# Values by 512-column products, and the scan branch's gates computed with features on partitions and turned back

## The chip, the cores and the metric

The kernel runs on one core of a Trainium2 chip. The time is the device time of one execution in microseconds (us). The profile has five engines: the tensor engine (PE, with its weight loads shown apart as PEld), the vector engine (DVE), the scalar engine (ACT), GpSimd (POOL) and the queue that issues transfers (SP). PSUM is the memory that the tensor engine writes its products to, in banks of 128 x 512 floats.

## The reference, cut to what matters

Three residual blocks run one after the other on one sequence of 1024 steps with 1024 features. The change touches one product in the first and one in the third:

```python
# block 1
u = jnp.einsum('bsd,de->bse', x, w_in) + b_in
q, k, v, z_att, glu_a, glu_b, z_conv, g_att, g_conv = jnp.split(u, _split_points(), axis=-1)
att = stick_breaking_attention(heads(q), heads(k), heads(v)).reshape(B, S, D_ATT)
c = glu_a * jax.nn.sigmoid(glu_b)
c = causal_depthwise_conv(c, conv_w, conv_b)          # 31 taps
...
# block 3
proj = hn @ w_in[i]
u_s5, z_s5, z_ssd, xBC, dt_raw = jnp.split(proj, SPLITS, axis=-1)
y_s5 = s5_branch(...) * jax.nn.silu(z_s5)
y_ssd = ssd_branch(xBC, dt_raw, z_ssd, ...)           # conv, chunked scan, y * silu(z_ssd), norm over groups of 256
h = h + jnp.concatenate([y_s5, y_ssd], axis=-1) @ w_out[i]
```

`v` has 512 features, `z_ssd` has 1024 in four groups of 256.

## The kernel before

All products are made in float32 accuracy from two parts of each operand, `hi` and `lo`, with three matmuls for each block of 128 features: hi x hi, hi x lo, lo x hi. A product over the 1024 features is therefore a chain of 24 matmuls into one PSUM bank. A weight comes by a transfer into `wraw` (2 buffers), ACT rounds it to `whi` (L146) and POOL subtracts to get `wlo` (L147); both have 3 buffers.

The usual product is `Core.dense`: a tile of 128 weight features is the stationary operand, half of time (512 steps) the moving one, so the result has features on partitions and time in the columns. All these matmuls stand under L156. `evac` takes the result out of PSUM, and `K.tick()` then writes the next steps of the background work into the program. Two products are made the other way round, with the activation as the stationary operand and time on partitions: the values `v` of block 1 (`projections`, L597, evacuated by DVE at L599) and the gates of block 3's scan branch (`SSD.rest`, L1670, evacuated by ACT at L1673 as `szt`, with a tanh into `zth` and the DVE operation L1676). Both run over 256 columns of weights at a time.

In `projections` the background work is the convolution over 31 taps: each tap is one DVE operation over 128 x 1024 (L568 on `co`). The stage runs over the convolution's inputs (evacuated at L557), q and k, then V, then two sets of gates (L608).

In block 3, the function `block3` goes through four groups g. The scan of a group (`SSD.scan`, 8 chunks of 128 steps) is written with high priority ahead of `SSD.project(g + 1)`, which makes the next group's inputs: `conv_in` (products, then a convolution of 4 taps on DVE, L1631 to L1639), then `rest`: the gates and the turning of the inputs (`xt`, `bt`) to time on partitions (transposes L1649). A chunk of the scan goes from POOL (`sg`, L1705) to PE (L1707), ACT (`M`), DVE (L1714), PE (L1720), DVE (L1723, L1727, L1728), POOL (L1742); the state passes through L1725. At a group's end DVE forms a norm (L1745, L1748), and for the first three groups `leaves` turns the result (four `turned` calls of 4 transposes, L1762), scales it by ACT into the one buffer `mo` (L1771) and sends it to memory (L1772). After the third group `glu` starts: it loads `gy` tiles (L1902; 2 buffers, tag "cp", which `conv_in` uses too), ACT and DVE split them (L70, L71), and products follow at L156.

All PE transposes write to the tag "tp", which has two PSUM banks. A bank is taken in the order in which the program is written, so a transpose written later can't take a bank ahead of one written earlier.

Of the kernel before, what the change touches and what calls it, by code (L numbers as in the profile page):

```python
# [26 lines left out]
def parts(x, bits):  # L27
    """x as three floats, the first two short enough that small multiples of them are exact."""
    a = float(np.float32(math.floor(x * 2.0 ** bits) / 2.0 ** bits))
    b = float(np.float32(math.floor((x - a) * 2.0 ** (bits + 10)) / 2.0 ** (bits + 10)))  # L30
    return a, b, float(np.float32(x - a - b))
# [14 lines left out]
class Act:  # L46
    """An activation, features on partitions, as float32r parts: n tiles, each by halves of time."""
# [14 lines left out]
    def scaled(self, k, h, src, scale, early=None):  # L62
        """The parts of src * scale, one factor for each feature. early: (t, a, b) with a t + b = src * scale, known before src."""
# [10 lines left out]
class Core:  # L74
    """Pools, constants and the pieces that all three blocks share."""
# [31 lines left out]
    def activation(self):  # L107
        """The activation that the products read next, in the place of the one before."""
        return Act(self, 8, "y", self.ypools)
# [19 lines left out]
    def weight(self, src, a, b, eng=None):  # L129
        """A weight tile [128, a, b] as two float32r parts that add up to it."""  # L130
# [5 lines left out]
    def warm(self, n):  # L136
        """Products of ones that keep the tensor engine's clock up until the first operands are there."""
# [11 lines left out]
    def mm3(self, ps, w, x, half, first=True, last=True, cols=slice(None)):  # L149
        """ps += sum over the k-tiles of w[k].T @ x[k] over one half of time or its columns cols, in float32 from the parts."""  # L150
# [16 lines left out]
    def dense(self, srcs, x, evac, group=1):  # L167
        """evac(index, half, psum) for each 128-feature tile of the product."""
        self.dense_list([(src, lambda hf, ps, i=i: evac(i, hf, ps)) for i, src in enumerate(srcs)], x, group)

    def dense_list(self, items, x, group=1):
        """evac(half, psum) for each (weight, evac); a group of tiles takes the first half of time, then the second."""
# [13 lines left out]
    def dense_half(self, srcs, x, evac, h, cols=slice(0, HALF), eng=None):  # L186
        """One half of time, or its columns cols, for all tiles; evac(index, psum)."""
# [9 lines left out]
    def tick(self):  # L197
        """Trace the next steps of the work that runs beside the products."""
# [7 lines left out]
    def tables(self, name):  # L206
        """From here on the activations that need a table use this set; those traced earlier go first."""
# [8 lines left out]
    def act(self, out, in_, func, **kw):  # L216
        """An activation with a function that not every table set has."""
# [5 lines left out]
    def in_turn(self, ins):  # L223
        """Keeps a step of the work that hooks trace behind the products that were traced before."""
# [4 lines left out]
    def rsqrt(self, pool, v, n):  # L229
        """v ** -0.5 for a small [128, n] tile, by Newton's iteration."""  # L230
# [15 lines left out]
    def exp(self, pool, x):  # L246
        """x = exp(x) in place for a small tile: 2 ** n from the exponent's bits, the rest from tanh."""
# [18 lines left out]
    def score_bank(self):  # L266
        """Three banks for attention scores where nothing needs sums over the features."""
# [3 lines left out]
    def stat_bank(self):  # L271
        """A bank for sums over the features; beside the attention's steps they have one of their own."""
# [4 lines left out]
    def col_sums(self, ps, at, accs, n=4):  # L277
        """ps[:, at + b] = the sum over partitions and tiles of acc[:, 128 b : 128 b + 128]."""
# [5 lines left out]
    def spread(self, pool, col, tag, n=4, bufs=2):  # L284
        """[128, n] with time on partitions -> [128, 128 n], the same row on each partition."""
# [8 lines left out]
    def inverse_rms(self, pool, accs, eps, dim, n=4):  # L294
        """(mean square + eps) ** -0.5 over the features, time on partitions."""
# [7 lines left out]
class Squares:  # L303
    """Squares of tiles added up, in two chains on two engines."""
# [23 lines left out]
class Norm:  # L328
    """h * g in parts, for products that take the norm's factor for each time step afterwards."""
# [18 lines left out]
def block1(K, hold, g0, then):  # L348
    """Returns h, the norm that block 2 starts from and what then(h, norm) gave, traced beside the end. hold: an ExitStack for what stays open."""
# [48 lines left out]
    if True:  # L398
        pl = left(el, "pl")
        lng, lnb = K.const("ln_g", (128, 8), pool=pl), K.const("ln_b", (128, 8), pool=pl)  # L400
        with ExitStack() as em:
# [43 lines left out]
            def finish(hf, engines=None):  # L445
                """Steps of the layer norm in place, and the next norm's factor: the mean of (r c g + b) ** 2 from sums over c g c g and 2 c g b."""
# [49 lines left out]
class LayerNorm:  # L496
    """(t - mean) * (variance + eps) ** -0.5 over the features, step by step for one stretch of time."""
# [40 lines left out]
def projections(K, pa, bin_, x, v):  # L538
    """The inputs of the convolution, the convolution itself, values and gates."""
# [47 lines left out]
    for c in range(2):  # L587
        wa, wb = K.weight(I["w_v"][c, 0], 4, 256), K.weight(I["w_v"][c, 1], 4, 256)
        for tb in range(8):
            ps = K.mm_bank()  # L590
            n = 0
            for k in range(8):
                wh, wl = (wa, wb)[k // 4]
                xh, xl = x.at(k, tb // 4)
                ts = slice(tb % 4 * 128, (tb % 4 + 1) * 128)
                for a, b in ((xh, wh), (xl, wh), (xh, wl)):
                    nc.tensor.matmul(ps[:, :256], a[:, ts], b[:, k % 4, :], start=n == 0, stop=n == 23)  # L597
                    n += 1
            nc.vector.tensor_add(v[:, tb, c * 256:(c + 1) * 256], ps[:, :256], bv[:, c * 256:(c + 1) * 256])  # L599
# [18 lines left out]
def conv_branch(K, pb):  # L618
    """What remains of the convolution's branch before its product, as steps that run beside the attention."""
# [168 lines left out]
def merge(K, pm, pz, m, cz, az):  # L788
    """m = the two branches' products, each under its gate."""
# [27 lines left out]
def even(K, h, norm, pe):  # L817
    """Traces the first tiles of the layer, for the first half of time; returns what traces the others."""
# [1324 lines left out]
```

## Time and profile before

| | |
|---|---|
| median of 3 runs | 3303.04 us |
| lowest and highest run | 3298.67, 3305.75 us |
| span of the profiled execution | 3303.1 us |
| PE busy | 3150.4 us, 95% |
| DVE busy | 2130.6 us, 65% |
| POOL busy | 1468.9 us, 44% |
| ACT busy | 1110.7 us, 34% |

The profiled execution agrees with the median. Its times are counted from the start of the span. A row "L597 <- wlo, x70h 128x256" is an instruction written at line 597 that reads these two tiles; "x3" are three in a row; the text in square brackets is the idle time of the engine just before, and what ended it. PE's matmuls are pipelined: the duration shown is longer than the step from one start to the next.

### The profile page before, as it was taken

The numbers are of one execution on the slowest core, as the hardware profiler recorded it, in microseconds if no ns is written. First come the engines' busy times: TensorE is split into PE (matmuls) and PEld (weight loads), VectorE is DVE, ScalarE is ACT, GpSimd is POOL, SyncE is SP. The second block draws the span as 40 slices with busy tenths as digits, with TensorE's granted clock in tenths as the row PEclk, the third lists the DMA queues.
The fourth block names the chain that finished last, engine by engine and source line by source line (L and its number), as shares of the span: only waits on it lengthen the run. The fifth ranks groups of instructions, "written<-read, shape, count | busy, mean of one in ns | idle before, by whom it ended". The sixth has DMA issues, their size and how long they took to land. (4 is left out here: it accounts for less than half of the span.)

```text
span 3303.1 us, 41709 instructions
## 1 busy us (share of the span) xinstructions
PE 3150.4 (95%) x15689; PEld 2522.8 (76%) x15689; DVE 2130.6 (65%) x3382; ACT 1110.7 (34%) x1974; POOL 1468.9 (44%) x1128
## 2 busy tenths in 40 slices
PE   9999999999989999999999999999999879989997
PEld 7877677778768888777777777787777768778886
DVE  8986887663773462232287777766955988874444
ACT  3025556553341121111144334521112323423343
POOL 2322332225644446777543222541214665794455
PEclk9999999999989999999999999999989999989999
DMA  3132122134311122122121111364253232365322
GB/s 128 52 107 78 68 77 76 47 136 140 110 64 45 42 69 68 56 89 75 51 74 42 42 36 65 135 190 127 88 130 93 76 104 71 118 223 182 115 91 100
DMA packets 159738, 303.95 MB, mean 92 GB/s; under 512 B 23840, under 2 KB 66864, under 8 KB 159536
## 3 DMA queue, kind: packets, MB, share of 16 engines
q1 hardware_dynamic: 149104, 294.96, 27.4%
q10 hardware_dynamic: 10368, 6.30, 0.9%
q8 instruction: 124, 2.03, 0.3%
q14 instruction: 78, 0.64, 0.1%
q0 software_dynamic: 64, 0.03, 0.0%
HBM read 236.59 MB, written 64.62 MB: 91 GB/s over the span
## 5 line engine op out<-in xcount | busy, mean ns | idle before, releaser
L147 POOL TENSOR_TENSOR wlo<-wraw,whi 128x1024 fp32r<-128x1024 f32 (+1 forms) x305 | 751.5, 2466 | 1086.2 <-ACT whi L146 1037.2
L146 ACT CAST whi<-wraw 128x1024 fp32r<-128x1024 f32 (+1 forms) x309 | 307.9, 998 | 806.4 <-PE mm L156 593.3
L568 DVE SCALAR_TENSOR_TENSOR co<-cpad,conv_w,co 128x1024 f32<-128x1024 f32 x120 | 180.3, 1543 | 0.9
L156 PE MATMUL mm<-mixh,whi 128*128 128x512 f32 x256 | 99.3, 393 | 2.1 <-DVE h L927 2.1
L156 PE MATMUL mm<-mixh,wlo 128*128 128x512 f32 x256 | 99.7, 391 | 0.0
L156 PE MATMUL mm<-mixl,whi 128*128 128x512 f32 x256 | 99.7, 391 | 0.0
L1636 DVE SCALAR_TENSOR_TENSOR h<-cp,conv_w,h 128x512 f32<-128x512 f32 x96 | 95.3, 993 | 3.3
L218 ACT ACTIVATE e<-e 128x128 f32<-128x128 f32 (+7 forms) x128 | 84.5, 681 | 33.5 <-DVE e L758 32.6
L762 DVE TENSOR_TENSOR_SCAN e<-e 128x128 f32<-128x128 f32 (+7 forms) x64 | 93.3, 1466 | 0.7
L927 DVE TENSOR_TENSOR h<-h,mm 128x512 f32<-128x512 f32 x64 | 43.3, 680 | 59.3 <-PE mm L156 59.3
L761 DVE TENSOR_TENSOR e<-e,z 128x128 f32<-128x128 f32 (+7 forms) x64 | 53.9, 851 | 37.3 <-ACT e L218 37.2
L320 DVE TENSOR_TENSOR sq<-sq,sq 128x512 f32<-128x512 f32 (+1 forms) x46 | 54.0, 1174 | 29.8 <-ACT sq L319 28.9
L1956 DVE TENSOR_TENSOR h<-h,mm 128x512 f32<-128x512 f32 x32 | 21.9, 684 | 76.2 <-PE mm L156 76.2
L832 DVE TENSOR_TENSOR sz<-mm,row 128x512 f32<-128x512 f32 x32 | 22.0, 689 | 75.0 <-PE mm L156 75.0
L218 ACT ACTIVATE z<-z 128x128 f32<-128x128 f32 (+7 forms) x64 | 43.3, 683 | 75.7 <-DVE z L763 75.6
L1720 PE MATMUL tp<-xd,M 128*128 128x64 f32 x256 | 38.6, 298 | 30.7 <-DVE M L1714 28.6
L1720 PEld LDWEIGHTS tp<-xd,M 128*128 128x128 f32 x256 | 36.0, 212 | 39.0 <-DVE M L1714 26.5
L916 DVE TENSOR_TENSOR cv<-mm,cv 128x512 f32<-128x512 f32 x16 | 11.1, 691 | 81.4 <-PE mm L156 81.4
L319 ACT ACTIVATE sq<-h 128x512 f32<-128x512 f32 x60 | 37.7, 629 | 72.2 <-POOL h L1988 29.7
L156 PE MATMUL mm<-y00h,whi 128*128 128x512 f32 x138 | 56.5, 410 | 3.9 <-DVE zt L1795 3.3
L1041 POOL TENSOR_TENSOR sw<-sw,rope_s 128x512 f32<-128x512 f32 x18 | 28.5, 1583 | 69.9 <-DVE sw L1040 65.9
L156 PEld LDWEIGHTS mm<-mixh,whi 128*128 128x128 f32 x256 | 48.1, 188 | 14.3 <-DVE h L927 2.8
(1524 smaller groups left out, 10533.7 us busy)
## 6 DMA issues: line engine op xcount, KB each, us to landing
wraw<-w_in SPq DMA_DIRECT2D x76, 512.0 KB, 3.6
wraw<-w_in_even SPq DMA_DIRECT2D x53, 512.0 KB, 3.5
wraw<-w_in_odd SPq DMA_DIRECT2D x22, 512.0 KB, 3.5
sp_g<-gt SPq DMA_DIRECT2D x32, 256.0 KB, 2.0
g<-sp_g SPq DMA_DIRECT2D x32, 256.0 KB, 3.1
wraw<-w_out SPq DMA_DIRECT2D x16, 512.0 KB, 3.4
wraw<-w_out_even SPq DMA_DIRECT2D x32, 256.0 KB, 2.6
wraw<-w_out_odd SPq DMA_DIRECT2D x16, 512.0 KB, 3.6
```

The source lines that it names most:

```text
L146: self.nc.scalar.copy(hi, src)
L147: (eng or self.nc.gpsimd).tensor_sub(lo, src, hi.bitcast(F32))
L156: ins = self.nc.tensor.matmul(ps, a[:, k, :], b[:, cols], start=first and n == 0, stop=last and n == total - 1).ins
L218: ins = self.nc.scalar.activation(out, in_, func, **kw).ins
L319: nc.scalar.activation(sq, src, AF.Square, scale=scale)
L320: (nc.vector if self.count > 5 else self.engines[i]).tensor_add(self.accs[i], self.accs[i], sq)
L568: nc.vector.scalar_tensor_tensor(o, cpad[:, tap:tap + S], cw[:, j, tap:tap + 1], o, op0=ALU.mult, op1=ALU.add)
L761: nc.vector.tensor_tensor(e[:, :L], e[:, :L], z[:, :L], op=ALU.max)
L762: nc.vector.tensor_tensor_scan(e[:, rev], e[:, rev], e[:, rev], 0.0, op0=ALU.add, op1=ALU.bypass)
L927: nc.vector.tensor_add(h[e][:, half(hf)], h[e][:, half(hf)], ps)
L1636: nc.vector.scalar_tensor_tensor(oh, c(d), cw[:, ch, 3 - d:4 - d], oh, op0=ALU.mult, op1=ALU.add)
L1720: nc.tensor.matmul(yp[:, i * 64:(i + 1) * 64], M[:, i, :], xd[:, i * 64:(i + 1) * 64], start=True, stop=True)
```

## The change

1. **Values.** The weights of V are laid out as four pieces of 256 input features by 512 output features. All four pieces, in both parts, stay in a pool of their own (`vw`). Eight products of 24 matmuls over 512 columns take the place of sixteen over 256. A product is evacuated by one DVE operation over 512 columns, followed by two `K.tick()`.
2. **Gates.** `rest` makes the gates with `K.dense`, two tiles of 128 features by two halves of time. For each of the four results ACT copies PSUM to `zf` (tag "cp"), PE turns it with 4 transposes into a "tp" bank, ACT takes the four blocks out with the time factor `zc`, then one tanh and one DVE operation over 512 columns follow. Buffers of the tags "cp" and "th" are used; `zth` is gone.
3. Docstrings are removed, which shifts line numbers. In block 3 a line of before is 6 lines further down in the changed kernel (L1762 is L1768, L1725 is L1731); the V product is at L603, the gates' transposes at L1674.

```diff
-    for c in range(2):
-        wa, wb = K.weight(I["w_v"][c, 0], 4, 256), K.weight(I["w_v"][c, 1], 4, 256)
+    with K.pool("vw") as vw:
+        wv = []
+        for q in range(4):
+            raw = K.wp.tile([128, 2, 512], F32, tag="wraw", name=K.n("wraw"), bufs=2)
+            hi, lo = (vw.tile([128, 2, 512], F32R, name=K.n("wv")) for _ in range(2))
+            nc.sync.dma_start(raw, I["w_v"][q])
+            K.split_into(raw, hi, lo)
+            wv.append((hi, lo))
         for tb in range(8):
             ps = K.mm_bank()
...
-                    nc.tensor.matmul(ps[:, :256], a[:, ts], b[:, k % 4, :], start=n == 0, stop=n == 23)
+                    nc.tensor.matmul(ps, a, b, start=n == 0, stop=n == 23)
                     n += 1
-            nc.vector.tensor_add(v[:, tb, c * 256:(c + 1) * 256], ps[:, :256], bv[:, c * 256:(c + 1) * 256])
+            nc.vector.tensor_add(v[:, tb, :], ps, bv)
+            K.tick()
             K.tick()
...
         sz = pool.tile([128, 8, 256], F32, tag="szt", name=K.n("szt"), bufs=2)
-        wz = [K.weight(K.I["w_z_3"][g, i], 4, 256) for i in range(2)]
-        for tb in range(8):
...
-                for p, q in ((xh, wh), (xl, wh), (xh, wl)):
-                    nc.tensor.matmul(ps[:, :256], p[:, ts], q[:, k % 4, :], start=n == 0, stop=n == 23)
-                    n += 1
-            z = sz[:, tb, :]
-            nc.scalar.activation(z, ps[:, :256], AF.Copy, scale=self.zc[:, tb:tb + 1])
-            t2 = pool.tile([128, 256], F32, tag="zth", name=K.n("zth"), bufs=2)
-            K.act(t2, z, AF.Tanh)
-            nc.vector.scalar_tensor_tensor(z, t2, 1.0, z, op0=ALU.add, op1=ALU.mult)
+
+        def ev(i, hf, ps):
+            z = self.pc.tile([128, 4 + HALF], F32, tag="cp", name=K.n("zf"), bufs=2)[:, 0:HALF]
+            nc.scalar.copy(z, ps)
+            pt = K.tp_bank()
+            for k in range(4):
+                nc.tensor.transpose(pt[:, k * 128:(k + 1) * 128], z[:, k * 128:(k + 1) * 128], K.ident)
+            o = sz[:, 4 * hf:4 * hf + 4, i * 128:(i + 1) * 128]
+            for k in range(4):
+                nc.scalar.activation(o[:, k, :], pt[:, k * 128:(k + 1) * 128], AF.Copy, scale=self.zc[:, 4 * hf + k:4 * hf + k + 1])
+            t2 = self.pc.tile([128, HALF], F32, tag="th", name=K.n("th"), bufs=2).rearrange("p (a b) -> p a b", b=128)
+            K.act(t2, o, AF.Tanh)
+            nc.vector.scalar_tensor_tensor(o, t2, 1.0, o, op0=ALU.add, op1=ALU.mult)
             K.tick()
+
+        K.dense([K.I["w_z_3"][2 * g + i] for i in range(2)], y, ev)
```

The change moves instructions at three places. POOL, first block, the weight splits around V: `wlo` are the splits of q's, k's and the gates' weights, and the two pairs wlo_774, wlo_780 and wlo_1027, wlo_1033 of before are V's. First before, then after, where V's are called `wv`.

```order
22 L147 TENSOR_TENSOR wlo_708<-wraw_706,whi_707 128x1024
23 L147 TENSOR_TENSOR wlo_774<-wraw_772,whi_773 128x1024
24 L147 TENSOR_TENSOR wlo_780<-wraw_778,whi_779 128x1024
25 L147 TENSOR_TENSOR wlo_1027<-wraw_1025,whi_1026 128x1024
26 L147 TENSOR_TENSOR wlo_1033<-wraw_1031,whi_1032 128x1024
```

```order
21 L147 TENSOR_TENSOR wlo_642<-wraw_640,whi_641 128x1024
22 L147 TENSOR_TENSOR wv_777<-wraw_775,wv_776 128x1024
23 L147 TENSOR_TENSOR wlo_708<-wraw_706,whi_707 128x1024
24 L147 TENSOR_TENSOR wv_783<-wraw_781,wv_782 128x1024
25 L147 TENSOR_TENSOR wv_789<-wraw_787,wv_788 128x1024
26 L147 TENSOR_TENSOR wv_795<-wraw_793,wv_794 128x1024
```

All four splits are still there, but the first now stands ahead of the last split before V, and all four stand ahead of V's first product.

PE, third block, the end of the second group's scan. Before, the first eight of the sixteen transposes of `leaves` (from `szt`) stand behind the start of a product; 21 matmuls of this product follow, then four transposes, eight matmuls of the next product and the last four transposes. These rows are the last two sets of transposes and what stands between them:

```order
11611 L1762 MATMUL tp_21649<-ident,szt_21033 128x128 x4
11612 L156 MATMUL mm_22792<-y01h_17411,whi_22730 128x512
11613 L156 MATMUL mm_22792<-y01l_17412,whi_22730 128x512
11614 L156 MATMUL mm_22792<-y01h_17411,wlo_22731 128x512
11615 L156 MATMUL mm_22792<-y11h_17415,whi_22730 128x512
11616 L156 MATMUL mm_22792<-y11l_17416,whi_22730 128x512
11617 L156 MATMUL mm_22792<-y11h_17415,wlo_22731 128x512
11618 L156 MATMUL mm_22792<-y21h_17419,whi_22730 128x512
11619 L156 MATMUL mm_22792<-y21l_17420,whi_22730 128x512
11620 L1762 MATMUL tp_21657<-ident,szt_21033 128x128 x4
```

After, behind the scan's last state product (L1731, row 11089) and four more rows like the first:

```order
11094 L1768 MATMUL tp_21276<-ident,szt_20753 128x128
11095 L1768 MATMUL tp_21285<-ident,szt_20753 128x128
11096 L1768 MATMUL tp_21276<-ident,szt_20753 128x128
11097 L1768 MATMUL tp_21285<-ident,szt_20753 128x128
11098 L1768 MATMUL tp_21293<-ident,szt_20753 128x128 x4
11099 L1768 MATMUL tp_21301<-ident,szt_20753 128x128 x4
11100 L1674 MATMUL tp_21690<-ident,zf_21688 128x128 x4
11101 L1674 MATMUL tp_21751<-ident,zf_21749 128x128 x4
11102 L156 MATMUL mm_22262<-y01h_17207,whi_22222 128x512
11103 L156 MATMUL mm_22262<-y01l_17208,whi_22222 128x512
```

The products between the transposes are gone: all sixteen transposes of `leaves` now follow each other, then eight of the next group's gates (`zf`), and only then a product. At the first group's end the order is the same but for seven matmuls ahead of L1768.

PE, third block, the end of the third group's scan in the changed kernel (L1726 and L1731 are scan steps; the product at 11425 is the first of `glu`; L1656 turns the fourth group's inputs):

```order
11416 L1731 MATMUL tp_22141<-st_22120,h_6307 128x256
11417 L1713 MATMUL aux_22855<-sg_22859,after_17710 128x512
11418 L1726 MATMUL tp_22178<-xd_22176,M_22169 128x64 x4
11419 L1674 MATMUL tp_22603<-ident,zf_22601 128x128 x4
11420 L1674 MATMUL tp_22664<-ident,zf_22662 128x128 x4
11421 L1674 MATMUL tp_22731<-ident,zf_22729 128x128 x4
11422 L1731 MATMUL tp_22178<-st_22157,h_6307 128x256
11423 L1674 MATMUL tp_22770<-ident,zf_22768 128x128 x4
11424 L1656 MATMUL tp_22784<-ident,h_6310 128x128 x4
11425 L156 MATMUL mm_23276<-y00h_23173,whi_23271 128x512
```

The last gate product of the fourth group ends at row 11409; from there to row 11425 PE has scan steps and transposes only. In the kernel before, `glu`'s products stand between the steps of the third scan.

## Rows read from the trace of the kernel before

**Rows 1.** Busy time by stretches of the span: length, then for each engine busy us (instructions), PE's granted clock, share and rate of the DMA engines.

```profile
94.90:153.70 58.80, 51.99 (x384) 51.05 (x384) 57.33 (x55) 4.20 (x4) 15.01 (x5) 0.88 0.16 54
153.70:233.00 79.30, 77.76 (x339) 62.57 (x337) 78.94 (x59) 15.91 (x21) 22.93 (x8) 1.00 0.26 90
2504.70:2873.10 368.40, 323.58 (x1840) 278.81 (x1840) 316.34 (x435) 124.59 (x250) 236.91 (x215) 0.95 0.26 88
```

**Rows 2.** Timeline of PE, instructions in order of start: start, duration, line, tiles. First and last of 8 matmuls of V that follow each other, first and last of 22 over 512 columns, and four transposes as one row.

```profile
109.76 0.28 PE L597 MATMUL mm<-wlo,x70h 128*128 128x256 f32 x1
110.60 0.28 PE L597 MATMUL mm<-whi,x20h 128*128 128x256 f32 x1
...
227.78 0.39 PE L156 MATMUL mm<-x01h,wlo 128*128 128x512 f32 x1
232.55 0.39 PE L156 MATMUL mm<-x71h,wlo 128*128 128x512 f32 x1
...
2660.47 0.60 PE L1649 MATMUL tp<-ident,h 128*128 128x128 f32 x4
```

**Rows 3.** The V stage and what follows: waits of PE from 94.9 to 153.8 us (total, times, longest); then timelines of DVE, of POOL, and of DVE and PE at the stage's end.

```profile
PE mm L597 <- POOL wlo L147: 3.6, 1, 3.6
PE mm L597 <- DVE v L599: 3.1, 2, 2.3
...
108.90 3.67 DVE L568 SCALAR_TENSOR_TENSOR co<-cpad,conv_w,co 128x1024 f32<-128x1024 f32 x3
128.57 3.07 DVE L568 SCALAR_TENSOR_TENSOR co<-cpad,conv_w,co 128x1024 f32<-128x1024 f32 x1
...
124.38 6.18 POOL L147 TENSOR_TENSOR wlo<-wraw,whi 128x1024 fp32r<-128x1024 f32 x2 [20.71 <-ACT whi L146]
...
232.22 1.40 DVE L608 SCALAR_TENSOR_TENSOR gt<-mm,b_in,gs 128x512 f32<-128x512 f32 x2
233.02 0.50 PE L156 MATMUL mm<-x00h,whi 128*128 128x512 f32 x1
```

**Rows 4.** DVE's groups of instructions by line and shape, in the projections (94.9 to 233 us) and in block 3's scans (2500 to 2985 us): count, total us, mean ns, idle time before them.

```profile
L568 DVE SCALAR_TENSOR_TENSOR co<-cpad,conv_w,co 128x1024 f32<-128x1024 f32 x80 | 122.6, 1571 | 0.4
L599 DVE TENSOR_TENSOR v<-mm,b_v 128x256 f32<-128x256 f32 x16 | 6.7, 417 | 1.4 <-PE mm L597 1.3
...
L1676 DVE SCALAR_TENSOR_TENSOR szt<-zth,szt 128x256 f32<-128x256 f32 x32 | 26.0, 816 | 10.5 <-ACT zth L218 10.3
L1639 DVE SCALAR_TENSOR_TENSOR h<-th,h 128x512 f32<-128x512 f32 x24 | 22.5, 936 | 3.7 <-ACT th L218 3.6
```

**Rows 5.** The end of the first two groups. For group 0 the scan's last state products, the transposes of `leaves` and DVE's L1748; then ACT's `mo` operations of group 0 and of group 1 (min/median/max ns, first and last start); one product of PE behind the idle time; and busy time by stretches as in rows 1, for groups 0 and 1.

```profile
L1725 PE MATMUL tp<-st,h x14: 377/379/634, 2565.9 to 2630.5; 128*128 128x256 f32 x14
L1762 PE MATMUL tp<-ident,szt x16: 270/273/476, 2643.8 to 2658.0; 128*128 128x128 f32 x16
2641.21 6.42 DVE L1748 TENSOR_SCALAR szt<-szt,rsq 128x256 f32<-128x256 f32 x8
L1771 ACT ACTIVATE mo<-tp,ssd_norm_w x4: 673/690/691, 2649.2 to 2661.4; 128x512 f32<-128x512 f32 x4
L1771 ACT ACTIVATE mo<-tp,ssd_norm_w x4: 669/690/692, 2772.5 to 2781.8; 128x512 f32<-128x512 f32 x4
2647.72 0.78 PE L156 MATMUL mm<-y00l,whi 128*128 128x512 f32 x1
...
2643.00:2661.00 18.00, 15.31 (x71) 12.60 (x72) 12.83 (x19) 5.07 (x8) 5.11 (x6) 0.91 0.47 160
2769.80:2782.00 12.20, 12.20 (x65) 10.21 (x64) 11.11 (x15) 3.77 (x7) 2.70 (x3) 1.00 0.30 108
```

**Rows 6.** First scan step on PE of groups 1 and 2 (first and last start of 16).

```profile
L1711 PE MATMUL tp<-h,h x16: 272/275/527, 2677.8 to 2748.3; 128*128 128x128 f32 x16
L1711 PE MATMUL tp<-h,h x16: 270/275/377, 2797.1 to 2852.1; 128*128 128x128 f32 x16
```

**Rows 7.** The third group's end: busy time of L71 alone (DVE, the splits of `gy`) from 2504.7 to 2873.1 us; the `gy` transfers; the scan's last state products and its norm L1745; the first `glu` products; and busy time by stretches as in rows 1.

```profile
2504.70:2873.10 368.40, 17.98 (x16) 0.95 0.26 88
L1902 SPq DMA_DIRECT2D gy<-sp_yg x16: 319/319/320, 2812.4 to 2867.3; - x16
DMA to landing us min/median/max: 2.4/2.5/2.6
L70 ACT ACTIVATE y00h<-gy x1: 619/619/619, 2829.0 to 2829.0; 128x512 fp32r<-128x512 f32 x1
L70 ACT ACTIVATE y70h<-gy x1: 632/632/632, 2847.1 to 2847.1; 128x512 fp32r<-128x512 f32 x1
L1725 PE MATMUL tp<-st,h x14: 377/379/483, 2820.2 to 2865.4; 128*128 128x256 f32 x14
L1745 DVE TENSOR_SCALAR ssv<-ss x1: 173/173/173, 2873.1 to 2873.1; 128x8 f32<-128x8 f32 x1
2854.43 0.40 PE L156 MATMUL mm<-y00h,whi 128*128 128x512 f32 x1
...
2865.40:2880.00 14.60, 12.56 (x62) 9.60 (x61) 11.15 (x25) 7.45 (x12) 6.65 (x4) 1.00 0.56 189
2880.00:2955.00 75.00, 65.89 (x298) 52.81 (x296) 51.35 (x63) 24.73 (x43) 67.33 (x55) 0.89 0.66 220
2955.00:2990.00 35.00, 35.00 (x164) 29.15 (x164) 22.87 (x37) 10.66 (x18) 25.64 (x16) 1.00 0.61 196
```

More of the change, by code (lines that the diff above doesn't have):

```diff
@@ L585, in projections @@
     K.dense_list(items[2:], x)
-    for c in range(2):
-        wa, wb = K.weight(I["w_v"][c, 0], 4, 256), K.weight(I["w_v"][c, 1], 4, 256)
+    with K.pool("vw") as vw:
[6 more added lines that the diff above has]
+            wv.append((hi, lo))
         for tb in range(8):
             ps = K.mm_bank()
+            ts = slice(tb % 4 * 128, (tb % 4 + 1) * 128)
             n = 0
             for k in range(8):
-                wh, wl = (wa, wb)[k // 4]
-                xh, xl = x.at(k, tb // 4)
-                ts = slice(tb % 4 * 128, (tb % 4 + 1) * 128)
+                wh, wl = (w[:, k % 2, :] for w in wv[k // 2])
+                xh, xl = (t[:, ts] for t in x.at(k, tb // 4))
                 for a, b in ((xh, wh), (xl, wh), (xh, wl)):
-                    nc.tensor.matmul(ps[:, :256], a[:, ts], b[:, k % 4, :], start=n == 0, stop=n == 23)
+                    nc.tensor.matmul(ps, a, b, start=n == 0, stop=n == 23)
                     n += 1
-            nc.vector.tensor_add(v[:, tb, c * 256:(c + 1) * 256], ps[:, :256], bv[:, c * 256:(c + 1) * 256])
+            nc.vector.tensor_add(v[:, tb, :], ps, bv)
+            K.tick()
             K.tick()
@@ L1660, in rest @@
         sz = pool.tile([128, 8, 256], F32, tag="szt", name=K.n("szt"), bufs=2)
-        wz = [K.weight(K.I["w_z_3"][g, i], 4, 256) for i in range(2)]
-        for tb in range(8):
-            ps = K.mm_bank()
-            n = 0
-            for k in range(8):
-                wh, wl = wz[k // 4]
-                xh, xl = y.at(k, tb // 4)
-                ts = slice(tb % 4 * 128, (tb % 4 + 1) * 128)
-                for p, q in ((xh, wh), (xl, wh), (xh, wl)):
-                    nc.tensor.matmul(ps[:, :256], p[:, ts], q[:, k % 4, :], start=n == 0, stop=n == 23)
-                    n += 1
-            z = sz[:, tb, :]
-            nc.scalar.activation(z, ps[:, :256], AF.Copy, scale=self.zc[:, tb:tb + 1])
-            t2 = pool.tile([128, 256], F32, tag="zth", name=K.n("zth"), bufs=2)
-            K.act(t2, z, AF.Tanh)
-            nc.vector.scalar_tensor_tensor(z, t2, 1.0, z, op0=ALU.add, op1=ALU.mult)
+        def ev(i, hf, ps):
[10 more added lines that the diff above has]
+            nc.vector.scalar_tensor_tensor(o, t2, 1.0, o, op0=ALU.add, op1=ALU.mult)
             K.tick()
+        K.dense([K.I["w_z_3"][2 * g + i] for i in range(2)], y, ev)
         t = [self.store[g % 2 * 4 + i] for i in range(4)]
@@ L2024, in host1 @@
     r["b_v"] = rep(np.asarray(a["b_in"])[0, 1024:1536])
-    wv = w[:, 1024:1536].reshape(2, 4, 128, 2, 256)
-    r["w_v"] = np.ascontiguousarray(wv.transpose(3, 0, 2, 1, 4))
+    r["w_v"] = np.ascontiguousarray(w[:, 1024:1536].reshape(4, 2, 128, 512).transpose(0, 2, 1, 3))
     r["conv_w"] = np.ascontiguousarray(np.asarray(a["conv_w"])[0].reshape(31, 4, 128).transpose(2, 1, 0))
@@ L2079, in host3 @@
     r["w_in_3"] = tiles(w[:, keep])
-    wz = w[:, 2048:3072].reshape(2, 4, 128, 4, 256)
-    r["w_z_3"] = np.ascontiguousarray(wz.transpose(3, 0, 2, 1, 4))
+    r["w_z_3"] = tiles(w[:, 2048:3072])
     r["w_dt_3"] = np.ascontiguousarray(w[:, 5120:].reshape(8, 128, 16).transpose(1, 0, 2))
```

## The prediction

> **What bounds the kernel now.** I read the busy time by stretches first, then waits and timelines where the change lies. PE is busy 95% of the span, but not in the two stages that change. In the V stage DVE is busy 57.33 of 58.80 us and in the gates after it 78.94 of 79.30 [rows 1]: it works through 80 taps of 1571 ns [rows 4]. That PE waits for it shows at the end: the first product at 233.02 starts when the DVE operations begun at 232.22 are through [rows 3]. So the projections end when DVE's list ends, and PE's waits inside (3.6 and 3.1 us, [rows 3]) are slack.
>
> In the scans of block 3, from the last operation of the branch before (2504.7) to the norm of the third group (2873.1), PE has 323.58 us of 368.40, DVE 316.34, POOL 236.91 [rows 1]. Neither is full: chunks of the scan go from engine to engine, and products and conv taps fill in between. The first group ends with a gap: the last state product is at 2630.5, the first transposes of `leaves` at 2643.8, because L1748 runs from 2641.21 [rows 5]. From 2955 PE has no gap (35.00 of 35.00, [rows 7]), and PE's work then sets the end. So block 3 comes down to how much PE work is left when PE becomes continuous.
>
> **PE's prices.** A 256-column matmul of V takes 0.84/7 = 0.120 us from start to start, one of 512 columns 4.77/21 = 0.227, a 128 x 128 transpose (0.60 - 0.27)/3 = 0.11 [rows 2]. V goes from 384 x 0.120 = 46.1 to 192 x 0.227 = 43.6: -2.5. The gates go from 768 x 0.120 = 92.2 to 384 x 0.227 = 87.2, plus 64 transposes at 7.0: +2.0. On PE's work alone the change is nothing, -0.5.
>
> **V.** DVE sets the stage, so its price counts: sixteen L599 of 417 ns, 6.7 us [rows 4], become eight over 512 columns. No row of this stage shows these; bounds are twice 417 ns (nothing saved) and the first of them unchanged (-3.3). A 512-column operation with PSUM input, L608 in [rows 3], takes 0.7 (two in 1.40), so 5.6: -1.1. With part of L599's 1.4 us of idle time [rows 4] I take -1.5, from 0 to -3. The POOL splits stay four. Each stretches a tap: 3.07 us beside a split (two run from 124.38) against 3.67 for three without one [rows 3], a loss of 1.9. The Trainium skill, "SBUF — State Buffer", on the shared port pair between DVE and GpSimd, has one operation holding the pair for its whole length and the other blocked; the stretched tap agrees. By that rule it is the number of splits that counts, and that does not change; but one split now stands ahead of the last split before V, and all four ahead of V's products. If these late taps held back the convolution's own inputs, the cost would be up to 4 x 1.9 = +7.6. I take none of it: the list of taps behind is never empty (idle 0.4 us in all, [rows 4]), so taps that lose time here are taps that would lose it later.
>
> **Block 3 up to the third group's norm: a ledger of DVE.** It has 316.3 us busy and 52 idle in 368.4 [rows 1].
> - Gates: 32 x 816 ns = 26.0 become 16 over 512 columns at the price of L1639, the same operation on that shape, 936 ns [rows 4]: 15.0. That is -11.1.
> - The splits L71 of `gy`, 18.0 us [rows 7], come before 2873 now. In the changed order the `gy` loads need the "cp" buffers that hold `zf`, whose transposes stand behind the third scan. So they move behind: -18.0.
> - The ends of groups 0 and 1: all sixteen transposes of `leaves`, then eight of `zf`, then products. The last `zf` bank is freed by the fourth `mo`, which comes 12.2 and 9.3 us after the first (2649.2 to 2661.4, 2772.5 to 2781.8), as `mo` has one buffer and each waits for its transfer [rows 5]. Before, PE worked 15.31 of 18.00 and 12.20 of 12.20 in there. Now it has nothing but transposes for about 13 us each time, and DVE gets no new products: of its 12.83 and 11.11 us there [rows 5], 4.6 are L1748 in group 0; I count 8 and 9 lost as new idle time, +17. The lower bound is 0 (DVE lives on a stock of conv taps), the upper 24.
> - The last two chunks of the third scan run with nothing beside them, and PE makes two conv tiles more before the first scan: about 3 each, +6 (0 to 10).
>
> This gives -11.1 - 18.0 + 17 + 6 = -6: the norm at 2867. A count by PE says otherwise. Between the `zf` transposes and the next scan's first step stand 107 products and 32 transposes, 24.3 + 3.5 us; with the 13 us and a few at half clock some 45 us pass from the first transposes to that step, against 2677.8 - 2643.8 = 34 and 2797.1 - 2769.8 = 27 before [rows 5, 6]. That is +11 and +18; against it the three scans, with fewer gate operations and taps beside them, have to shrink by as much. If they give back 20 of 29, the norm is 10 late. I take 0 between -6 and +10.
>
> **Behind the third scan.** Up to the last state product the kernel before has 708 gate matmuls and 610 of 512 columns on PE (85.0 + 138.5 = 223.5 us), the changed one 916 of 512 columns and 60 transposes (207.9 + 6.6 = 214.5): 9 us of PE work move behind, mostly `glu`, which began at 2854.43, ahead of the last state product at 2865.4 [rows 7]. Added idle time: from the `zf` transposes a `gy` load has to be issued and land (2.5), and pass ACT (0.6), before a product: with issue and DVE's part 5. Then eight loads through two buffers, 18.1/7 = 2.6 apart (2829.0 to 2847.1, [rows 7]), for 9 matmuls of 0.227 = 2.04 each: 8 x 0.55 = 4. Before, PE idled 2.0 + 9.1 = 11.1 us from 2865.4 to 2955 [rows 7]; the work that is now later fills about half, -5. Sum: 9 + 5 + 4 - 5 = +13 (from 5 to 20).
>
> **Sum.** -1.5 + 0 + 13 = +11.5, on the profiled execution's 3303.1, which is the median: 3314.6, some 3314.
>
> **Rivals.**
> 1. *Faster: the DVE work that is gone comes through.* The ends of groups cost no DVE time, since conv taps in stock fill them, the ledger stands at -29 + 6 = -23 at 2873, and the +13 behind it leave -10; with -1.5 to -3 for V: about 3291. For it: 52 us of idle time on DVE are room to absorb a 13 us gap. Against it: L1636's input comes from products, and PE has none. It decides if the first step of the second scan starts before 2680.
> 2. *No change.* PE's work is the same within 0.5 us, and the gaps only change places: what is lost at the ends of groups returns in shorter scans, and the 11 us of idle time after 2865 takes all of the 9: 3299 to 3308.
> 3. *Much slower: clock.* After the gap in group 0 a product took 0.78 us where 0.39 is usual, and the stretch was granted 0.91 [rows 5]. The gaps are now longer, twice, and once more behind the third scan. Should the 107 products after each gap run at half of 2.4 GHz, each would take up to 0.227 longer, 24 a gap; a third of that in three places, 24 in all, gives 3335. The Trainium skill, "TensorE: Matmul & The Clock Gate", part 4 on PE-mode transposes, says a transpose does not count as work for the clock: by that the 24 transposes do not help to hold it. That the first gap's stretch lost only about 2 us (18 x 0.09) speaks against the size.
> 4. *Slower by V.* The early splits hold the convolution back by the 7.6 us above: 3322 with the rest.
> 5. *V does what PE's row promises.* If DVE's list had slack, PE would save its waits and the half-clock stretch: 58.8 - 43.6 = -15, so 3301. DVE's 57.33 of 58.80 leaves no room, I give it little.
>
> **Chances.** Forecast (3308 to 3322) 0.42; rival 1 0.23; rival 2 0.20; rival 3 0.09; rival 4 0.05; rival 5 0.01. The runs of this kernel differ by 0.2%, which is what can be told from no change: 6.6 us, 3296.4 to 3309.7. Faster by more takes rival 1, 0.23; inside fall rivals 2 and 5 and a small part of the forecast, 0.24; slower 0.53. The range leaves out the tails of rivals 1 and 3: 3290 to 3332.
>
> **What the changed profile would show.** V: DVE still full from 95 to the end of the gates, which ends at 231 to 233; V's matmuls 0.227 apart. Wrong if the gates end over 3 us away from there. Groups: some 13 us without products behind the first two scans, the second and third scan's first steps 45 us behind the first transposes; L1680 at about 0.94 us; the scans shorter by 6 to 20 us each. Third group: its norm between 2867 and 2883, `glu`'s first product behind the last state product and not ahead of it, PE without gaps from about 2960. The forecast fails if DVE has enough stock to run through the gaps (rival 1), or if the clock falls for long (rival 3).

## The result

The changed kernel takes 3329.58 us (median of 4 runs, 3327.79 to 3331.67) against 3303.83 (4 runs of the kernel before on the same chip): ratio 1.0083, 95% interval 1.0069 to 1.0098, so +26 us. Measured once more beside other kernels it stands at 1.0080 (1.0067 to 1.0092). The forecast was 3314, with 3290 to 3332 as its range: slower as forecast, by more than twice as much. The profiled execution has a span of 3326.0 us, 22.9 more than that of before.

First the V stage and the gates behind it: busy time by stretches (columns as in rows 1), PE's wait, twelve taps on DVE while the weights are split (before, then after the change), DVE's evacuations of V, the first V matmul and the first one of the gates, and the 16 evacuations of the gates (first and last start; before, then after).

```profile
94.90:149.70 54.80, 54.80 (x238) 44.36 (x237) 54.77 (x48) 1.88 (x3) 16.67 (x2) 1.00 0.09 29
149.70:231.20 81.50, 78.19 (x336) 62.26 (x336) 80.92 (x65) 14.75 (x19) 19.06 (x6) 1.00 0.25 85
...
PE mm L156 <- DVE cpad L557: 8.6, 1, 8.6
...
59.00 18.70 DVE L568 SCALAR_TENSOR_TENSOR co<-cpad,conv_w,co 128x1024 f32<-128x1024 f32 x12
58.60 27.23 DVE L568 SCALAR_TENSOR_TENSOR co<-cpad,conv_w,co 128x1024 f32<-128x1024 f32 x12
...
L605 DVE TENSOR_TENSOR v<-mm,b_v 128x512 f32<-128x512 f32 x8 | 5.5, 689 | 0.0
...
104.95 0.40 PE L603 MATMUL mm<-wv,x00h 128*128 128x512 f32 x1
149.75 0.39 PE L156 MATMUL mm<-x00h,whi 128*128 128x512 f32 x1
...
L608 DVE SCALAR_TENSOR_TENSOR gt<-mm,b_in,gs x16: 736/742/755, 164.9 to 245.8; 128x512 f32<-128x512 f32 x16
L615 DVE SCALAR_TENSOR_TENSOR gt<-mm,b_in,gs x16: 735/744/755, 163.0 to 244.0; 128x512 f32<-128x512 f32 x16
```

DVE is as full as in [rows 1]: 54.77 of 54.80 and 80.92 of 81.50. PE's waits inside V [rows 3] and the clock of 0.88 [rows 1] are gone, but PE has an 8.6 us wait ahead of V in their place: twelve taps take 27.23 us instead of 18.70, and the input that the convolution and PE need comes behind them. V starts at 104.95, 10 us later than before (94.9), so the first stretch also holds products that stand ahead of V. The last of the 16 evacuations starts at 244.0 instead of 245.8: 1.8 us come through.

Now block 3: from the last DVE operation of the branch before (2502.1; before 2504.7) to the norm of the third group, and from there to the first DVE addition of the output products. The kernel before has its first stretch in [rows 1]; here is its second, then the two of the changed kernel and DVE's time on L71 in the first of them.

```profile
2873.10:2997.10 124.00, 113.40 (x520) 91.96 (x519) 84.35 (x122) 43.94 (x72) 98.85 (x72) 0.93 0.61 203
```

```profile
2502.10:2878.70 376.60, 319.33 (x1470) 258.74 (x1471) 276.38 (x402) 123.15 (x263) 229.32 (x215) 0.89 0.23 74
2878.70:3019.20 140.50, 127.76 (x580) 104.85 (x580) 106.35 (x138) 53.89 (x90) 104.80 (x73) 0.92 0.62 211
...
2502.10:2878.70 376.60, 1.23 (x1) 0.89 0.23 74
```

The two stretches are 8.2 and 16.5 us longer, 24.7 in all. DVE has 40 us less to do in the first, and it ends later all the same: its idle time goes from 52 to 100 us. Behind the output products both kernels run alike.

The end of the second group shows what PE lacks. PE, ACT and DVE there (the scan's last state products are L1731; L1768 turns the group's result, L1674 the next group's gates); then the busy time by stretches there, and that of the kernel before from its last state products to the transposes; last, the first transposes and the first product at the end of the first group:

```profile
2761.49 0.70 PE L1731 MATMUL tp<-st,h 128*128 128x256 f32 x2 [0.59 <-DVE yo L1729]
2767.48 1.94 PE L1768 MATMUL tp<-ident,szt 128*128 128x128 f32 x8 [5.29 <-DVE szt L1754]
2769.98 1.11 PE L1768 MATMUL tp<-ident,szt 128*128 128x128 f32 x4 [0.56 <-ACT mo L1777]
2772.84 1.11 PE L1768 MATMUL tp<-ident,szt 128*128 128x128 f32 x4 [1.75 <-ACT mo L1777]
2775.68 1.11 PE L1674 MATMUL tp<-ident,zf 128*128 128x128 f32 x4 [1.73 <-ACT mo L1777]
2778.03 1.11 PE L1674 MATMUL tp<-ident,zf 128*128 128x128 f32 x4 [1.23 <-ACT szt L1677]
2778.80 0.77 PE L156 MATMUL mm<-y01h,whi 128*128 128x512 f32 x1
...
2772.11 0.69 ACT L1777 ACTIVATE mo<-tp,ssd_norm_w 128x512 f32<-128x512 f32 x1 [2.17 <-DMA sp_mb<-mo]
2774.94 0.69 ACT L1777 ACTIVATE mo<-tp,ssd_norm_w 128x512 f32<-128x512 f32 x1 [2.15 <-DMA sp_mb<-mo]
...
2766.98 2.19 DVE L1754 TENSOR_SCALAR szt<-szt,rsq 128x256 f32<-128x256 f32 x8
2779.60 0.69 DVE L1680 SCALAR_TENSOR_TENSOR szt<-th,szt 128x512 f32<-128x512 f32 x1 [10.43 <-ACT th L218]
...
2761.80:2778.80 17.00, 6.44 (x27) 4.48 (x25) 5.06 (x22) 4.62 (x12) 0.72 (x1) 0.55 0.12 46
2757.00:2769.80 12.80, 12.80 (x63) 10.70 (x62) 9.34 (x27) 4.38 (x8) 6.13 (x4) 1.00 0.25 82
...
2638.76 1.94 PE L1768 MATMUL tp<-ident,szt 128*128 128x128 f32 x8 [10.95 <-DVE szt L1754]
2652.79 0.78 PE L156 MATMUL mm<-y01h,whi 128*128 128x512 f32 x1
```

For 17 us PE has no product: it waits 5.29 us for the norm and is then held up between transposes. Each later set of transposes waits for ACT to free a bank, ACT waits for the transfer out of `mo`, and DVE stands still for 10.43 us. In the same place PE of the kernel before was busy without a gap (12.80 of 12.80, and behind it 12.20 of 12.20 [rows 5]). The granted clock is 0.55, half of 2.4 GHz most of the time, and the first product behind the gap takes 0.77 us where 0.39 is usual. At the end of the first group it is longer: some 25 us without a product, 14.0 of them from the first transposes (2638.8) to the first product (2652.8).

### The profile page after: what moved, and what is told of

It reads as the page before. It is cut to its first block, busy times and chain, and to the rows that moved or that the text cites. A ratio compares the mean times of both kernels' runs of the same rounds, so it can differ in the third digit from the quotient of the medians.

```text
span 3326.0 us, 40740 instructions
## 1 busy us (share of the span) xinstructions
PE 3155.6 (95%) x15177; PEld 2500.1 (75%) x15177; DVE 2114.4 (64%) x3358; ACT 1119.7 (34%) x2006; POOL 1467.7 (44%) x1128
## 5 line engine op out<-in xcount | busy, mean ns | idle before, releaser
L147 POOL TENSOR_TENSOR wlo<-wraw,whi 128x1024 fp32r<-128x1024 f32 (+1 forms) x301 | 741.4, 2464 | 1117.9 <-ACT whi L146 1070.7
L923 DVE TENSOR_TENSOR cv<-mm,cv 128x512 f32<-128x512 f32 x16 | 11.1, 692 | 81.4 <-PE mm L156 81.4
L156 PE MATMUL mm<-y01h,whi 128*128 128x512 f32 x146 | 59.5, 409 | 2.9 <-ACT y01h L68 2.4
L156 PE MATMUL mm<-y01h,wlo 128*128 128x512 f32 x146 | 59.6, 409 | 1.2 <-POOL wlo L147 1.2
L156 PE MATMUL mm<-y01l,whi 128*128 128x512 f32 x146 | 60.5, 414 | 0.3 <-DVE y01l L71 0.3
L156 PE MATMUL mm<-y30l,whi 128*128 128x512 f32 x146 | 58.0, 398 | 2.1 <-DVE y30l L71 2.1
```

The costliest lines, as they stand in the source:

```text
L147: (eng or self.nc.gpsimd).tensor_sub(lo, src, hi.bitcast(F32))
L156: ins = self.nc.tensor.matmul(ps, a[:, k, :], b[:, cols], start=first and n == 0, stop=last and n == total - 1).ins
```

## The experiments

Ratios are to the kernel before on the same chip, with 95% intervals.

**The two halves apart.** The values' change in the kernel before (e1), and the gates' change alone (e2): each is the diff of the change without its other part.

> Only the values are changed; the gates are as before. If DVE's list sets the stage, the time falls by 0 to 3 us (3301 to 3304), the gates of the first block end at 231 to 233 us, and nothing moves behind. If the early splits hold the convolution back, it is 3307 to 3311. If the gates' change and the values' change only cost together, it stands elsewhere.

> Only the gates are changed; the values are as before. If the gates' change carries the loss, 3328 to 3333 (+25 to +28, what the whole change lost plus the little that the values gave). If the loss came in the first block, 3303 to 3308.

e1: 3301.52, 0.9999 (0.9989 to 1.0008). e2: 3319.32, 1.0055 (1.0037 to 1.0072). The values are worth nothing that can be measured; the gates carry the loss. But e2 is 10 us faster than both parts together, though e1 is no slower than before. Block 3 alone, from the last DVE operation of the branch before to the first addition of the output products, in e1 (its two stretches, parted at the norm) and in e2:

```profile
2501.20:2875.50 374.30, 333.56 (x1857) 286.91 (x1858) 310.52 (x435) 126.00 (x252) 241.76 (x216) 0.94 0.27 86
2875.50:2994.50 119.00, 110.74 (x506) 90.71 (x505) 86.46 (x122) 43.16 (x70) 96.75 (x72) 0.91 0.63 211
...
2497.20:3011.80 514.60, 441.83 (x2049) 358.55 (x2050) 377.95 (x539) 176.25 (x352) 334.29 (x288) 0.91 0.35 112
```

Before, block 3 takes 492.4 us, in e1 493.3, in e2 514.6, in the changed kernel 517.1 and in its second profile (e5) 519.5. So there the gates alone cost 22 us of 25 to 27. Of the 8.9 us between the profiles of e2 and of the changed kernel, 4.9 are there before block 3 begins (2497.2 against 2502.1). This point moves between executions anyway: in e9 it lies at 2498.7 and in e6 at 2508.1, with the code of the changed kernel up to there. Whether the values add a few us to the gates' loss stays open.

**A bank of their own for the gates' transposes (e3).**

```diff
-            pt = K.tp_bank()
+            pt = K.pp.tile([128, HALF], F32, tag="stat", name=K.n("zp"), bufs=1)
```

> The whole change, but the gates' transposes go to a PSUM bank of their own (tag stat, which nothing uses during the scans) and no longer wait for the two banks of the scan. If the wait for these banks is the cause (products missing at the ends of the groups, glu behind the third scan), the transposes move into the scans, products stand between those of leaves again, glu starts before 2865, and the time is 3294 to 3306. If the loss is the work itself (64 transposes, 80 more ACT operations, the shared cp and th buffers), it stays above 3320.

3302.41, 0.9998 (0.9989 to 1.0007): all of the loss is gone with one line, though all 64 transposes, the ACT operations and the shared buffers are still there. PE in the place of the 17 us gap, then the two stretches of block 3:

```profile
2774.54 1.03 PE L1768 MATMUL tp<-ident,szt 128*128 128x128 f32 x8
2775.33 0.48 PE L156 MATMUL mm<-y21l,whi 128*128 128x512 f32 x1
...
2779.99 0.39 PE L156 MATMUL mm<-y10h,whi 128*128 128x512 f32 x1
2780.22 0.60 PE L1768 MATMUL tp<-ident,szt 128*128 128x128 f32 x4
...
2500.70:2876.30 375.60, 338.73 (x1594) 272.30 (x1594) 298.31 (x420) 137.87 (x286) 245.54 (x220) 0.96 0.28 89
2876.30:2995.90 119.60, 105.47 (x456) 84.66 (x457) 78.85 (x122) 38.72 (x67) 90.24 (x69) 0.86 0.63 204
```

Between the sets of transposes products of the next group run one behind the other, 0.23 us apart. The norm comes as late as in the changed kernel (375.6 and 376.6 us), but the stretch behind it is 20.9 us shorter, as `glu` starts at 2829.2, during the third scan: the time of the norm alone does not tell what is lost. The edit also gives the transposes one bank more. A third bank for the shared tag was not tried, so the order and the number of banks are not told apart.

**A buffer of its own for `zf` (e4).** `zf` takes the tag "zf" with one buffer in place of "cp" with two.

> The whole change, but zf has one buffer of its own in place of the two that the convolution's input and the gy loads use too. The order at the scan's banks stays. If the shared buffers are the cause, the convolution's first operations and the gy loads no longer wait for the gates' transposes, and the time is 3305 to 3315. If the order at the banks is the cause, products still can't go on behind the third bank of PSUM, and with one buffer the gates come later: 3325 to 3340.

3342.96, 1.0123 (1.0103 to 1.0143): worse. The convolution and the `gy` loads no longer share buffers with the gates, and nothing is gained. But with one buffer the gates also wait for each other, so this run alone can't say what the sharing costs. e3 says more: the buffers are shared there too, and with the transposes out of the scan's banks that costs nothing.

**The clock (e6), beside the changed kernel again (e5).**

```diff
+    def fill(self, n):
+        ps, xh = self.K.pp.tile([128, HALF], F32, tag="stat", ...), self.norm.y.at(0, 0)[0]
+        for k in range(n):
+            ins = self.K.nc.tensor.matmul(ps, xh[:, 0:128], xh, start=k == 0, stop=k == n - 1).ins
```

> The changed kernel itself once more, beside the next three on one chip, as the values' and the gates' changes did not add up (+16 for the gates alone against +26 for both). If the two do interact, it stays at 3325 to 3332; if the 26 held some of a difference between chips, 3316 to 3322.

> The changed kernel with products that nobody reads, on PE at the ends of the first two groups: 20 ahead of the transposes of leaves and 8 behind each of the first three sets, into a bank that is free; the order is otherwise that of the changed kernel. PE then works where it idled, and its clock stays up. If the clock behind the gaps is the main cause, the time falls by 10 to 13 us (half-clock products of 512 columns are 65 more than before, at 0.2 us each). If the gaps cost by the missing products themselves, only the 20 half-clock products right behind them come back: -2 to -5.

e5: 3328.47, 1.0080; e6: 3326.77, 1.0073 (1.0061 to 1.0085). The same group's end in e6, PE and busy time:

```profile
2765.04 4.90 PE L1780 MATMUL fill<-y00h 128*128 128x512 f32 x20
2778.44 0.66 PE L1674 MATMUL tp<-ident,zf 128*128 128x128 f32 x4
2780.80 0.50 PE L156 MATMUL mm<-y01h,whi 128*128 128x512 f32 x1
...
2765.00:2781.00 16.00, 14.00 (x71) 10.99 (x70) 5.06 (x22) 4.86 (x13) 0.74 (x1) 1.00 0.13 50
```

PE works through the gap, the clock is 1.00 and the products behind start at full rate; 1.7 us come back, not told from zero by the intervals. In block 3 alone the profile has 513.3 us, against 517.1 and 519.5 (e5), so the clock is worth a few us at most, and the added products delay nothing (the first transposes stand as far behind the last state products as in the changed kernel). What costs is mainly that no useful product runs there.

**The last group (e7).** The fourth group's gates as before the change (256 columns, L1670's code), the others as after it.

> The changed kernel, but the fourth group's gates are made in the old way, so that glu can begin beside the third scan. If the late glu costs what the trace shows behind the third group's norm (16 us), the time falls by 12 to 18 us against the changed kernel; the two earlier ends of groups keep some 8. If the late start of glu is filled by other work, nothing changes.

3329.2, 1.0083 (1.0069 to 1.0097): no gain, against my expectation of 12 to 18. The first `gy` tile is split at 2856.0, during the third scan, 21 us earlier than in the changed kernel. But its first product on PE comes at 2876.70, where the changed kernel has 2876.88 (4 us earlier if counted from the branch before): until then PE works on the fourth group's gates, now beside the third scan. So the edit does not bring `glu`'s products forward, and it does not test what their lateness costs. Its two stretches are 380.5 and 135.6 us, where the changed kernel has 376.6 and 140.5. The first product of `glu` in this run and in the changed kernel, then the stretches of this run:

```profile
2876.70 0.48 PE L156 MATMUL mm<-y00h,whi 128*128 128x512 f32 x1
2876.88 1.63 PE L156 MATMUL mm<-y00h,whi 128*128 128x512 f32 x3
...
2505.80:2886.30 380.50, 322.65 (x1590) 264.85 (x1591) 290.11 (x419) 126.55 (x267) 230.70 (x215) 0.91 0.26 80
2886.30:3021.90 135.60, 116.78 (x542) 95.94 (x541) 90.63 (x126) 47.38 (x78) 99.94 (x73) 0.92 0.62 200
```

**Two buffers for `mo` (e8).**

```diff
-        o = pool.tile([128, HALF], F32, tag=tag, name=K.n("mo"), bufs=1)
+        o = pool.tile([128, HALF], F32, tag=tag, name=K.n("mo"), bufs=2 if tag == "mo" else 1)
```

> The changed kernel with two buffers for mo, so that the four steps of leaves no longer wait for each other's transfers. The eight transposes of zf come 5 to 7 us earlier at each of two ends. If these gaps are on the path, -6 to -12 against the changed kernel; if DVE or POOL set the pace anyway, under 3.

3314.26, 1.0039 (1.0026 to 1.0052): 14 us come back, a little more than I gave it. Two `mo` operations now follow each other, and the wait of the gates' transposes shrinks:

```profile
2766.14 1.27 ACT L1777 ACTIVATE mo<-tp,ssd_norm_w 128x512 f32<-128x512 f32 x2 [4.71 <-PE tp L1768]
...
2764.37 1.94 PE L1768 MATMUL tp<-ident,szt 128*128 128x128 f32 x8 [5.28 <-DVE szt L1754]
2773.26 0.78 PE L156 MATMUL mm<-y01h,whi 128*128 128x512 f32 x1
...
2503.70:2867.90 364.20, 315.51 (x1469) 256.41 (x1469) 279.52 (x400) 120.99 (x260) 231.68 (x215) 0.91 0.24 76
```

From the first transposes to the first product it is 8.9 us where the changed kernel has 11.3, and the norm comes 364.2 us behind the branch before, not 376.6. The next scan's first step follows the first transposes by 34.1 and 33.3 us, where the changed kernel has 45.0 and 41.6: that is more than the products gain, and why is not shown.

**The own bank for groups 0 to 2 only (e9).** As e3, with `if g < 3 else K.tp_bank()`.

> As the kernel with a bank of its own for the gates' transposes, but only for groups 0 to 2; the fourth group's still wait for the scan's banks and stand behind the third scan, so glu begins late as in the changed kernel, while the ends of the first two groups have their products back. If the ends of the first two groups are the cause and the time lost behind the third scan is only PE work that they left over: 3302 to 3309. If the late glu costs by itself what I gave it (13 us): 3312 to 3320.

3307.43, 1.0018 (1.0009 to 1.0026). `glu`'s first product stands 6 us behind the third scan's last state product here (2856.5 and 2850.1), 4 us later than in the changed kernel (2876.9 and 2874.9). So the ends of the first two groups cost about 20 of the 26 us, the late `glu` about 6. Its two stretches:

```profile
2498.70:2855.00 356.30, 313.72 (x1462) 250.25 (x1462) 277.95 (x399) 118.30 (x254) 230.55 (x215) 0.94 0.24 78
2855.00:2998.40 143.40, 131.16 (x600) 106.32 (x600) 99.97 (x142) 57.97 (x99) 102.34 (x74) 0.93 0.63 207
```

With `glu` late but the groups' ends whole, the norm comes 356.3 us behind the branch before, 20 earlier than in the changed kernel and 12 earlier than before the change; the stretch behind takes 143.4, 19 more than before.

**A version that beats both?** Own bank and two `mo` buffers (e10); the kernel before with two `mo` buffers, `zth` moved to the tag "th" to make room (e11); e11 with the values' change (e12).

> Own bank for the gates' transposes and two buffers for mo: does it beat both kernels? With products between the transposes of leaves the wait for mo is covered, so -1 to -4 against the own bank alone, 3298 to 3302. If mo holds back the next scan even there: 3290 to 3296.

> The kernel before with two buffers for mo (the tanh of the gates takes the tag th to make room). In the kernel before, products cover the wait for mo: 0 to -3, so 3299 to 3303. If mo paces the ends of the groups there as in the changed kernel, -10.

> The kernel before with the values' change and two buffers for mo, that is, what the runs so far leave standing: the gates as before. If the values' 1.5 to 3 us add to the 3.5 of the two buffers, 3293 to 3297; if the gain of either is lost in the scans behind it, 3297 to 3302.

e10: 3301.76, 1.0006 (0.9993 to 1.0018). e11: 3296.79, 0.9989 (0.9981 to 0.9998). e12: 3303.04, 0.9996 (0.9985 to 1.0006). Only e11 stands apart from the kernel before, by 0.1%, and e12, which differs from it by the harmless half, does not repeat it. e11's block 3, where its whole edit lies:

```profile
2493.30:2984.60 491.30, 439.30 (x2358) 373.92 (x2359) 400.64 (x556) 168.89 (x321) 336.90 (x287) 0.94 0.36 117
```

That is 1.1 us less than before (492.4); the rest of its shorter profile (3290.5) lies ahead of block 3, where the code is the same. Where products cover the wait for `mo`, a second buffer is worth 0 to 4 us by the medians and some 1 us by the profiles.

## Why the prediction was right or wrong

The mechanism forecast for the ends of the groups was right, and the size was short by more than half: +11.5 against +26. That 3329.58 lies inside 3290 to 3332 is luck: it is outside 3308 to 3322, and the upper edge came from rival 3, the clock, which e6 shows to be worth a few us at most.

- **V, right.** It gave 1.8 us in the profile where I took 1.5, and e1 does not tell it from nothing. An evacuation over 512 columns took 689 ns (0.7 estimated). The early splits did hold back the convolution's inputs and so PE (8.6 us ahead of V), but not DVE's end: the mechanism of rival 4 appeared and its price did not. Rival 5 falls with DVE at 54.77 of 54.80. The sign that I took for PE's wait at the stage's end was read too strongly: the product at 233.02 starts behind the first of the two DVE operations, only 0.2 us late [rows 2, 3]. The better sign is that V came 10 us later and the gates ended no later.
- **Gates on DVE, right in the sum and wrong in its worth.** L1680 took 16.1 us for 16 (15.0 forecast), and L71 left the first stretch (17.98 to 1.23). DVE's work there fell by 40 us, 11 more than counted; single groups of operations with nothing about them changed move by 6 us between profiles (last section).
- **The ends of the groups, right.** About 13 us without products were forecast for each, from the first transposes on; it is 14.0 and 11.3 (27 and 17 from the last state products). From the first transposes to the next scan's first step it takes 45.0 and 41.6 us (2638.8 to 2683.8, 2767.5 to 2809.1), forecast 45. Their price was forecast at 17; e9 against the changed kernel gives 20. e3 and e8 show that the banks of the transposes and the transfers of `mo` set it.
- **The step that failed: DVE work booked as time (-11.1 and -18.0), and with it "I take 0 between -6 and +10".** Two counts disagreed, and I put the middle. Block 3 was to lose 13 us up to the output products and lost 24.7 in the profile (22 in e2, 27 in e5). Against the profile of before, 8.2 of that stand at the norm, where I put 0. That the sum came near the second count's +10 is luck, as its parts are others: the first scan starts 6.8 later; the scans, from first step to last state product, are 8.9, 1.7 and 2.5 shorter (94.6 to 85.7, 79.7 to 78.0, 68.3 to 65.8; forecast 6 to 20 each), 13.1 in all; what follows a scan's last state product, up to the transposes or the norm, is 0.3, 6.6 and 3.9 shorter; and from the transposes to the next first step it is 11.0 and 14.3 longer. The scans gave back 13 where I said 20, the steps behind them 11 that I had not counted.
- **What holds in its place.** One pair of profiles can't settle how the loss divides at the norm: e1, whose block 3 is that of before, has 374.3 and 119.0 us where before has 368.4 and 124.0, and against e1 only 2.3 stand at the norm and 21.5 behind it. What both comparisons share is the sum (24 us), and that the work taken from DVE gave no time back. DVE's idle time was to go from 52 to 75 us; it went to 100. And e3, which has no gaps, takes 495.2 us for block 3 with 377.2 us of DVE work; the kernel before takes 492.4 with 400.7. So nothing came to set against the 17 us for the ends of the groups. That fits a stage paced by the scans' chain over five engines, which DVE work taken from beside it shortens little; no run tests this by itself.
- **Behind the third scan.** +13 forecast, +16.5 in the trace against before, but not for the reasons given alone. e9 has the late `glu` without the gaps: 12 us less ahead of the norm and 19 more behind it, 7 net, and 6 in the medians. So the late `glu` by itself costs about half of what I gave it, and by this difference most of what the changed kernel loses behind the norm is PE work that the two gaps left over; that is argued from sums, as e7 does not start `glu`'s products earlier.
- **Rivals.** Rival 1 fails on what it was to be decided by: the second scan's first step comes at 2683.8, not before 2680. Rival 2's time is that of e3, but for another reason: there the gaps are gone, while rival 2 has them made good elsewhere, which the changed kernel does not do. Rival 3 named a real thing of the wrong size: in the gaps the clock drops (0.55, and the transposes of L1768 take 421 ns there, 273 before [rows 5]), but e6 gives 1.7 us for it. The rule of the Trainium skill cited there ("TensorE: Matmul & The Clock Gate", part 4) fits this drop. But PE was busy for only 6.44 of the 17 us, so no run tells what the transposes do to the clock from what the idle time does. Rival 3's sum was also off: 24 on top of 3314.6 is 3338.6, not 3335.

## What to carry to other kernels

Two buffers that rotate in the order of the program tie everything written later to what was written earlier. A small helper step that borrows them (a transpose here) can drag whole products behind a serial tail, so give background work a buffer that the urgent chain doesn't turn, and look in the listing for places where the filler is gone. A ledger of one engine's work says little of a stage in which that engine is not full (DVE 316 of 368 us): when two counts of the same stretch disagree, find out which of the two paces it rather than take the middle. And before a difference of a few us in a profile is explained, look at how far the same mark moves where nothing was changed.

## Not expected of the hardware

Two of DVE's operations in the scans look shorter after the change, with nothing about them changed. Its groups over all of block 3 (busy time, mean ns, idle time), the kernel before and then the changed one:

```profile
L1714 DVE TENSOR_TENSOR M<-M,cm 128x512 f32<-128x512 f32 x32 | 43.6, 1363 | 0.6
L1717 DVE TENSOR_TENSOR xd<-xt,dt 128x256 f32<-128x256 f32 x32 | 25.8, 816 | 0.1
```

```profile
L1720 DVE TENSOR_TENSOR M<-M,cm 128x512 f32<-128x512 f32 x32 | 39.3, 1229 | 1.6
L1723 DVE TENSOR_TENSOR xd<-xt,dt 128x256 f32<-128x256 f32 x32 | 20.7, 658 | 0.0
```

Over all four groups that is 9.4 us less DVE work that no step of the ledger had. But it can't be put down to the change. The first of them in e1, whose block 3 is that of before, and the second in e9, whose block 3 has the new gates:

```profile
L1721 DVE TENSOR_TENSOR M<-M,cm 128x512 f32<-128x512 f32 x32 | 37.9, 1184 | 0.7
L1723 DVE TENSOR_TENSOR xd<-xt,dt 128x256 f32<-128x256 f32 x32 | 26.6, 842 | 2.4 <-PE tp L1726 2.4
```

So these sums move by 6 us from one profile to the next whatever the gates do. What is unexpected is how much one and the same operation varies: over 128 x 256 it takes 407 to 1895 ns in the kernel before. What else runs beside it differs; no run separates the cause.
